# A decoder step on one core: where Pool sums the convolution's results

## The chip, the cores and the metric

The kernel runs on one core of a Trainium2 chip. The core has five engines that work side by side, each through its own instructions in their order: TensorE (PE) for matrix products, VectorE (DVE), ScalarE (ACT) and Pool (GpSimd) for elementwise work, and SyncE (SP), which here only issues transfers (DMAs). The metric is the time of one execution on the device in microseconds, the lower the better.

## The reference

One inference step of a hybrid decoder with two layers, served to a prompt group (512 positions) and a sample group (8 sequences of 4 positions) that share the weights. The model width is 1024. Layer 0 mixes with a Conformer convolution, layer 1 with an S5 state-space scan; each layer goes on with a cross-attention to memory keys and values and an MLP. The change lies in the mixer of layer 0:

```python
def _conformer_conv(u, buf, w_in, b_in, dw, dw_b, ln_g, ln_b, w_out):
    h = jnp.einsum('bld,de->ble', u, w_in) + b_in
    g = h[..., :D_MODEL] * jax.nn.sigmoid(h[..., D_MODEL:])
    padded = jnp.concatenate([buf.astype(g.dtype), g], axis=1)
    c = lax.conv_general_dilated(padded, dw[:, None, :], ...) + dw_b   # depthwise, width 31
    mu = jnp.mean(c32, axis=-1, keepdims=True)
    var = jnp.mean(jnp.square(c32 - mu), axis=-1, keepdims=True)
    n = (c32 - mu) * lax.rsqrt(var + EPS) * ln_g + ln_b
    s = jax.nn.silu(n)
    return jnp.einsum('bld,de->ble', s, w_out), padded[:, -CONV_BUF:]
```

Beside it stand `k = mem @ w_k` and `v = mem @ w_v` for both layers, whose results are outputs too; they hang on nothing in the mixer.

## The kernel before

Activations lie with channels on the 128 partitions and 544 columns (512 prompt positions and 32 sample positions) in the free dimension, so the 1024 channels are eight tiles, numbered 0 to 7. Every product is made exact to fp32 by splitting weight and activation into a high and a low half and adding three products. A weight block (128x1024) lands in one of six `wst` tiles; `prep_block` copies its high half on ACT (L137) into one of three `whl` tiles and makes the low half by a subtraction at L177, on DVE or, for the blocks named in `lpool`, on Pool. The blocks of the first projection (`ldma`) instead get their low half by an adding DMA that Pool issues (L175).

The convolution layer is a list of steps, one after another, in the order of the string `PLAN`. `a4`, `b4` are the two projections of channel tile 4 on PE, `g4` its gate. Tiles 1, 2, 4, 5 and 7 are then convolved on PE by Toeplitz matrices: `f4` fetches the tile in another layout, `40` to `43` are its four Toeplitz products (L682), and `r4` gathers the result from DRAM by four DMAs (L672). The matrices are built on Pool (L655), into two buffers in turn: the products of one step issue the building of the matrix for the step after next. Tiles 0, 3 and 6 are convolved on DVE, tap by tap in PSUM (L702), in portions that the numbers in brackets grant. The sample positions of every tile are multiplied on Pool (L632). `k` is a step of the memory's keys and values (L450, L467), which fills PE meanwhile.

Each of the results of tiles 0 to 6 is added into the tile `acc` on Pool by `conv_sum` (L622 for the first, L624 for the others), and the call stands right behind the DMAs of the gather, or behind the last instruction of a tile on DVE. The result of tile 7 is not added.

`L1` is the first step of the LayerNorm. `layernorm1` sums `acc` and the result of tile 7 over the channels by a product with ones (L714); DVE then subtracts the mean from the eight tiles (L723), ACT squares them, and Pool and DVE sum the squares (L729, L735). `L1b`, `L2`, `L2b` and `L3` go on with it, with `k` steps in between. `run` readies weight blocks ahead of the step that uses them: as a rule two, at a step with `deep=1`, as `L1`, three, before the step's own instructions are issued, if a `whl` tile is free. At `L1` the third tile is that of the `k` step just before.

Of the kernel before, what the change touches and what calls it, by code (L numbers as in the profile page):

```python
# [57 lines left out]
class Trunk:  # L58
# [7 lines left out]

    PLAN = """
        k S k s k g0 F a1 (4.2) b1 (1.5) g1 f1 a2 (4.2) b2 (1.5) g2 10 (1.8) f2 11 (1.8) a3 (4.2) 12 (1.8) b3 (1.5) g3 13 (1.8) r1 20 (1.8)
        a4 (4.2) 21 (1.8) b4 (1.5) g4 22 (1.8) f4 a5 (4.2) 23 (1.8) b5 (1.5) g5 r2 40 (1.8) f5 a6 (4.2) 41 (1.8) b6 (1.5) g6 42 (1.8)
        43 (1.8) a7 (4.2) r4 50 (1.8) b7 (1.5) g7 51 (2) f7 52 (2) V k (2) 53 k (2) r5 70 (2) k (2) 71 (2) k (2) 72 k 73 r7 k k k L1 k L1b W k k L2 k L2b O L3 k E """  # L70

    def __init__(self, nc, tc, pool, psum, I, O):
        self.nc, self.tc, self.I, self.O = nc, tc, I, O
# [429 lines left out]
    def conv_layer(self):  # L503
        nc, I, O = self.nc, self.I, self.O
        self.gp = [None] * KT
        self.nacc = 0
        self.tg, self.td = {}, {}
        st = {}
        kvb = self.mm[2]
# [61 lines left out]
        def ln1():  # L571
            while self.bgq:
                self.pop_first()
            self.layernorm1()

        def end():
# [7 lines left out]
        S = self.steps  # L584
# [9 lines left out]
        def outs():  # L594
            for f in self.late:
                f()
            self.unhold(st["v"])

        named = {"O": outs, "L1b": self.layernorm1b, "V": vbank, "F": free, "W": vbank2, "L1": ln1, "L2": self.layernorm2, "L2b": self.layernorm2b, "L3": self.layernorm3, "E": end, "S": start_stat, "s": start_rstd}
        for u in self.PLAN.split():  # L600
            if u in named:
                S.append(Step(named[u], deep=int(u in ("L1", "L1b", "L3"))))
# [8 lines left out]
            else:  # L611
                w, i = (u[0], int(u[1])) if u[0] in "fr" else (int(u[1]), int(u[0]))
                S.append(Step(lambda w=w, i=i: self.toep(w, i)))
        assert not fill

    def conv_sum(self, i, g, eng):
        self.gp[i] = g
        self.nacc += 1
        if i == 7:
            return  # L620
        if self.nacc == 1:
            self.nc.gpsimd.tensor_copy(self.acc, g)  # L622
        else:
            eng.tensor_add(self.acc, self.acc, g)  # L624

    def samples(self, i, gw, prod):

# [16 lines left out]
    def toep(self, what, i, q=None):  # L644


        nc = self.nc
# [10 lines left out]
        if what == "f":  # L658
# [3 lines left out]
            up, y, g = self.slot(), self.slot(), self.slot()  # L662
# [6 lines left out]
        elif what == "r":  # L669
            up, y, g, prod = self.td.pop(i)  # L670
            for q in range(4):
                nc.sync.dma_start(self.tv(g[32 * q : 32 * q + 32])[:, :, 8:],  # L672
                                  self.yd[i][:, :512].rearrange("(a r) (q j) -> q r a j", a=4, q=4)[q])
            self.conv_sum(i, g, nc.gpsimd)
        else:
            q = what
            n = order.index((i, q))
            up, y, g, prod = self.td[i]
            o = self.aux[1][:, q * 128 : q * 128 + 128]
            x = up[:, q * 128 : q * 128 + 128]  # L680
            for s in range(9):
                nc.tensor.matmul(o[:, s:], mat(n)[:, s * 128 : s * 128 + 128], x[:, : 128 - s], start=s == 0, stop=s == 8)  # L682
            build(n + 2)
            self.act(y[:, q * 128 : q * 128 + 128], o, AF.Identity, bias=tp(i)[:, 144 + q : 145 + q])
            if q == 1:
                self.samples_sum(i, g, prod)
            if q == 3:
                nc.scalar.dma_start(self.yd[i][:, :512], y[:, :512])

    def conv_tile(self, i, g, gw):  # L690

        nc = self.nc
# [6 lines left out]
        out = self.slot()  # L699
# [3 lines left out]
            yield 0.7  # L703
        self.samples_sum(i, out, prod)
        self.act(self.tv(out)[:, :, 8:], A.rearrange("p (c a) -> p a c", a=4), AF.Identity, bias=self.v(V_DWB + i))
        self.conv_sum(i, out, nc.gpsimd)
        yield 1.3

    def layernorm1(self):
# [1525 lines left out]
```

## Time and profile before

| | |
|---|---|
| median of 3 runs | 1545.18 us (1544.69 to 1546.54) |
| the profiled execution's own time | 1544.75 us |
| its span in the trace | 1543.0 us |
| PE busy | 1496.6 us (97%) |
| DVE busy | 1015.6 us (66%) |
| ACT busy | 685.0 us (44%) |
| Pool busy | 200.9 us (13%) |

The span is the trace's own measure from the first to the last instruction; 1.75 us of the execution lie around it. The convolution layer, with the filling `k` steps, lies in the first 220 us or so. In the rows further down a time in brackets is the idle time of an engine just before an instruction, and the name behind the arrow what ended it.

### The profile page before, as it was taken

The page shows a single profiled execution, that of the slowest core. Times are in us where ns is not written, and L with a number is a line of the kernel's source. Part 1 is how long each engine was busy: PE and PEld are TensorE (multiplying, and loading weights), DVE is VectorE, ACT ScalarE, POOL GpSimd, SP SyncE. Part 2 cuts the span into 40 slices and gives each one's busy share as a digit, 9 for nine tenths or more (in the row PEclk, how much of TensorE's full clock was granted, in tenths as well). Part 3 has the DMA queues.
Part 4 walks back from the last instruction along what each step waited for, and adds up shares of the span by engine and source line. Part 5 has one row for each costly group of instructions (what it writes and reads, how often), then busy time and mean ns, then how long its engine had stood idle before and what let it go on. Part 6 is the DMA issues. An engine that isn't in the chain of part 4 may idle for free.

```text
span 1543.0 us, 29397 instructions
## 1 busy us (share of the span) xinstructions
PE 1496.6 (97%) x11949; PEld 1450.0 (94%) x11949; DVE 1015.6 (66%) x2094; ACT 685.0 (44%) x1274; POOL 200.9 (13%) x167
## 2 busy tenths in 40 slices
PE   8999979999999999999999999999999999999996
PEld 8999969898999999999998899998899999999996
DVE  6896786444576666666757964553479677685855
ACT  6332354343445433665443443343357445272642
POOL 2555550000000000000103750000000000000001
PEclk9999989999999999999999999999999999999998
DMA  8765526453223344433587974237322314141211
GB/s 278 191 156 136 185 82 219 150 220 133 101 83 103 134 134 134 134 134 116 170 271 226 340 237 182 110 138 271 125 69 85 135 55 151 42 146 47 92 46 59
DMA packets 92535, 224.49 MB, mean 145 GB/s; under 512 B 12496, under 2 KB 42976, under 8 KB 88304
## 3 DMA queue, kind: packets, MB, share of 16 engines
q1 hardware_dynamic: 87440, 211.06, 40.1%
q0 software_dynamic: 1792, 6.37, 2.3%
q10 hardware_dynamic: 3168, 5.18, 0.9%
q8 instruction: 94, 1.54, 0.4%
q14 instruction: 41, 0.34, 0.1%
HBM read 192.78 MB, written 29.80 MB: 144 GB/s over the span
## 4 chain that ended last, share of the span: by engine, by line
PE 78%; DVE 8%; ACT 1%; issue 1%; DMA 1%; POOL 0%; SPq 0%; DVEq 0%; POOLq 0%; ACTq 0%
PE banks L215 44%; PE banks L1403 12%; PE banks L1295 10%; PE banks L467 2%; PE banks L956 2%; PE banks L892 2%; PE banks L973 1%; PE banks L876 1%; PE banks L227 1%; PE banks L1382 1%; DVE banks L1958 1%; ACT slot L137 1%; DVE banks L702 1%; PE banks L1992 1%; PE banks L1780 0%
## 5 line engine op out<-in xcount | busy, mean ns | idle before, releaser
L215 PE MATMUL banks<-slot,whl 128*128 128x272 f32 x6264 | 805.0, 290 | 6.1 <-ACT slot L137 2.9
L215 PEld LDWEIGHTS banks<-slot,whl 128*128 128x128 f32 x6264 | 794.0, 189 | 11.4 <-ACT slot L137 4.8
L137 ACT ACTIVATE whl<-wst 128x1024 fp32r<-128x1024 f32 (+1 forms) x236 | 218.7, 930 | 132.8 <-PE banks L1403 47.8
L177 DVE TENSOR_TENSOR whl<-wst,whl 128x1024 fp32r<-128x1024 f32 x137 | 169.6, 1242 | 92.8 <-ACT whl L137 91.0
L1403 PE MATMUL banks<-slot,whl 128*128 128x272 f32 x912 | 120.2, 288 | 0.5 <-DVE rt L1316 0.5
L137 ACT ACTIVATE slot<-banks 128x512 fp32r<-128x512 f32 (+7 forms) x132 | 60.3, 480 | 135.5 <-PE banks L215 42.3
L1403 PEld LDWEIGHTS banks<-slot,whl 128*128 128x128 f32 x912 | 116.7, 188 | 0.7 <-DVE rt L1316 0.7
L1295 PE MATMUL banks<-slot,whl 128*128 128x272 f32 x756 | 97.2, 288 | 0.9 <-DVE tmp L1413 0.9
L1295 PEld LDWEIGHTS banks<-slot,whl 128*128 128x128 f32 x756 | 95.6, 188 | 1.1 <-ACT whl L137 1.1
L137 ACT ACTIVATE slot<-x,vec 128x544 fp32r<-128x544 f32 (+2 forms) x50 | 35.2, 727 | 108.7 <-DVE x L2027 43.8
L1413 DVE TENSOR_TENSOR tmp<-banks,rb 128x544 f32<-128x544 f32 x30 | 21.7, 724 | 83.0 <-PE banks L1403 83.0
L1403 PE MATMUL banks<-slot,arena_mlp 128*128 128x272 f32 x528 | 71.5, 288 | 0.4 <-DVE rt L1316 0.4
L1485 POOL MEMSET slot<- 128x128 f32 x1 | 0.2, 205 | 546.9 <-PE banks L1295 546.9
L702 DVE SCALAR_TENSOR_TENSOR banks<-slot,vec,banks 128x512 f32<-128x512 f32 x90 | 67.9, 755 | 2.8
L1403 PEld LDWEIGHTS banks<-slot,arena_mlp 128*128 128x128 f32 x528 | 68.2, 188 | 0.6 <-DVE rt L1316 0.6
L1295 PE MATMUL banks<-slot,arena_mlp 128*128 128x272 f32 x504 | 65.3, 288 | 0.4 <-DVE acc L1330 0.4
L1295 PEld LDWEIGHTS banks<-slot,arena_mlp 128*128 128x128 f32 x504 | 63.9, 188 | 0.7 <-DVE acc L1330 0.6
L137 ACT ACTIVATE tmp<-x 128x544 f32<-128x544 f32 x40 | 25.9, 648 | 65.0 <-DVE x L1099 39.7
L425 POOL TENSOR_TENSOR slot<-slot,slot 128x512 fp32r<-128x512 f32 x4 | 6.1, 1557 | 371.4 <-ACT slot L137 371.4
L137 ACT ACTIVATE tmp<-banks 128x544 f32<-128x544 f32 x32 | 19.9, 623 | 76.5 <-PE banks L215 76.5
L177 POOL TENSOR_TENSOR whl<-wst,whl 128x1024 fp32r<-128x1024 f32 x19 | 45.2, 2383 | 55.2 <-ACT whl L137 55.2
L250 DVE TENSOR_TENSOR slot<-tmp,slot 128x544 fp32r<-128x544 f32 x32 | 23.2, 726 | 41.5 <-ACT slot L137 41.5
(283 smaller groups left out, 2068.8 us busy)
## 6 DMA issues: line engine op xcount, KB each, us to landing
wst<-in_w SPq DMA_DIRECT2D x231, 512.0 KB, 4.4
arena_att<-in_kc SPq DMA_DIRECT2D x16, 1024.0 KB, 4.9
arena_att<-in_vc SPq DMA_DIRECT2D x16, 1024.0 KB, 5.3
tab<-arena_prep SPq DMA_DIRECT2D x24, 512.0 KB, 3.9
whl<-in_w POOLq DMA_DIRECT2D x12, 512.0 KB, 6.2
arena_s<-tab SPq DMA_DIRECT2D x8, 768.0 KB, 5.5
arena_s<-tab SPq DMA_DIRECT2D x8, 512.0 KB, 6.3
arena_s<-tab SPq DMA_DIRECT2D x12, 256.0 KB, 5.2
```

Of the source, the lines that this page charges most:

```text
L137: self.nc.scalar.activation(out, in_, func, **kw)
L177: eng.tensor_sub(t[:, 1].bitcast(F32R), src, t[:, 0])
L215: self.nc.tensor.matmul(ps[:, c, :HALF], w, x[:, c * HALF : c * HALF + HALF], start=first and n == 0, stop=last and n == len(seq) - 1)
L227: self.nc.tensor.matmul(ps[:, c, :HALF], self.w8(b, kt)[wi], rhs[kt][xi].bitcast(F32R)[:, c * HALF : c * HALF + HALF], start=first and kt ...
L250: self.nc.vector.tensor_sub(l.bitcast(F32R), src_h if src_l is None else src_l, h)
L467: nc.tensor.matmul(ps[m], self.memt(2 * kp + k2, xi)[:, m * 128 : m * 128 + 128], t[:, wi, k2 * 512 : k2 * 512 + 512], start=kp == 0 and k ...
L702: nc.vector.scalar_tensor_tensor(A, win(k), w(k), A, op0=ALU.mult, op1=ALU.add)
L892: nc.tensor.matmul(o, qs[qi], ks[ki], start=e == 0 and i == 0, stop=e == 1 and i == 2)
L956: nc.tensor.matmul(ps[e], vs[vi], xs[xi], start=m == 0 and i == 0, stop=m == 1 and i == 2)
L1295: nc.tensor.matmul(bank, u[:, wi, k * 128 : k * 128 + 128], x[k][xi].bitcast(F32R), start=n == k == 0, stop=n == 2 and k == 3)
L1403: nc.tensor.matmul(ps[:, c, :HALF], us[kt // 4][:, wi, kt % 4 * 128 : kt % 4 * 128 + 128], M["h"][kt][xi].bitcast(F32R)[:, c * HALF : c * ...
L1413: job("V", 0.7, lambda: V.tensor_mul(self.c2(t), self.psv(ps), self.c2(self.rb)), [*bk, "rb"], [("t", o % 2)])
```

## The change

`conv_sum` is replaced by `conv_sums`. Where a result was added into `acc` at once, it is now put on a list, `pend`, and the adds for all that is on the list are issued where `PLAN` has a new mark, `+`, and once more at the beginning of `L1`. There are three marks: before `f4`, before `a7`, and behind `53`. The number of instructions is the same on every engine, and the results are added in the same sequence as before (tiles 0, 1, 3, 2, 4, 5, 6).

```diff
-        a4 (4.2) 21 (1.8) b4 (1.5) g4 22 (1.8) f4 a5 (4.2) ...
-        43 (1.8) a7 (4.2) r4 50 (1.8) b7 (1.5) g7 51 (2) f7 52 (2) V k (2) 53 k (2) r5 70 (2) k ...
+        a4 (4.2) 21 (1.8) b4 (1.5) g4 22 (1.8) + f4 a5 (4.2) ...
+        43 (1.8) + a7 (4.2) r4 50 (1.8) b7 (1.5) g7 51 (2) f7 52 (2) V k (2) 53 + k (2) r5 70 (2) k ...
@@ def ln1
             while self.bgq:
                 self.pop_first()
+            self.conv_sums()
             self.layernorm1()
@@ 
-    def conv_sum(self, i, g, eng):
-        self.gp[i] = g
-        self.nacc += 1
-        if i == 7:
-            return
-        if self.nacc == 1:
-            self.nc.gpsimd.tensor_copy(self.acc, g)
-        else:
-            eng.tensor_add(self.acc, self.acc, g)
+    def conv_sums(self):
+        for i, g in self.pend:
+            self.gp[i] = g
+            if i == 7:
+                continue
+            self.nacc += 1
+            if self.nacc == 1:
+                self.nc.gpsimd.tensor_copy(self.acc, g)
+            else:
+                self.nc.gpsimd.tensor_add(self.acc, self.acc, g)
+        self.pend = []
@@ toep, step "r"
-            self.conv_sum(i, g, nc.gpsimd)
+            self.pend.append((i, g))
@@ conv_tile, its end
-        self.conv_sum(i, out, nc.gpsimd)
+        self.pend.append((i, out))
```

Only Pool's order changes; below, a line number of the changed kernel is that of before plus 3 to 4. The first place is Pool around `L1`. `slot_1313` (after: `slot_1311`) is the result of tile 5, `slot_1464` (`slot_1462`) that of tile 6; the three L177 are the low halves of the value blocks of the three `k` steps behind `L1`. Before:

```order
L624 TENSOR_TENSOR acc<-acc,slot_1313 128x544
L655 TENSOR_TENSOR arena_mem<-istk,slot_233 128x1152
L624 TENSOR_TENSOR acc<-acc,slot_1464 128x544
L655 TENSOR_TENSOR arena_mem<-istk,slot_233 128x1152
L177 TENSOR_TENSOR whl_81<-wst_78,whl_81 128x1024
L177 TENSOR_TENSOR whl_82<-wst_79,whl_82 128x1024
L177 TENSOR_TENSOR whl_83<-wst_80,whl_83 128x1024
L719 MEMSET slot_1968 128x256
```

Here both adds stood ahead of the last two matrices, and so ahead of the three low halves. After:

```order
L659 TENSOR_TENSOR arena_mem<-istk,slot_233 128x1152 x2
L177 TENSOR_TENSOR whl_81<-wst_78,whl_81 128x1024
L177 TENSOR_TENSOR whl_82<-wst_79,whl_82 128x1024
L177 TENSOR_TENSOR whl_83<-wst_80,whl_83 128x1024
L627 TENSOR_TENSOR acc<-acc,slot_1311 128x544
L627 TENSOR_TENSOR acc<-acc,slot_1462 128x544
L723 MEMSET slot_1968 128x256
L733 TENSOR_TENSOR acc<-acc,slot_1961 128x544
```

Both adds now stand behind all three low halves, the last of which is readied at `L1` itself.

The second place is TensorE at the same step, with what each instruction waits for. Before, the last products of the `k` step and the first of the LayerNorm's:

```order
L467 MATMUL banks<-whl_83,arena_mem 128x512
L467 MATMUL banks<-whl_83,arena_mem 128x512 [waits DVE_49]
L467 MATMUL banks<-whl_83,arena_mem 128x512 x9
L714 MATMUL banks<-acc,ones 128x272
L714 MATMUL banks<-slot_1645,ones 128x272 [waits DMAHW6_49,DMAHW7_49,DMAHW5_49,DMAHW0_49]
```

The product on `acc` had no wait of its own. After:

```order
L467 MATMUL banks<-whl_83,arena_mem 128x512
L467 MATMUL banks<-whl_83,arena_mem 128x512 [waits DVE_49]
L467 MATMUL banks<-whl_83,arena_mem 128x512 x9
L718 MATMUL banks<-acc,ones 128x272 [waits Pool_49]
L718 MATMUL banks<-slot_1644,ones 128x272 [waits DMAHW6_49,DMAHW7_49,DMAHW5_49,DMAHW0_49]
```

The product on `acc` now waits for Pool.

The third place is Pool between `43` and `70`, where `slot_1143` is the result of tile 4. Before:

```order
L655 TENSOR_TENSOR arena_mem<-istk,slot_233 128x1152
L624 TENSOR_TENSOR acc<-acc,slot_1143 128x544
L655 TENSOR_TENSOR arena_mem<-istk,slot_233 128x1152 x2
L632 TENSOR_TENSOR slot_1646<-slot_242,vec 128x496
L632 TENSOR_TENSOR slot_1647<-slot_242,vec 128x496
L655 TENSOR_TENSOR arena_mem<-istk,slot_233 128x1152 x2
```

The add of tile 4 stood between the matrices of the second and third product of tile 5. After, from the last matrix ahead of the second mark on (`slot_960` and `slot_782` are the results of tiles 3 and 2):

```order
L659 TENSOR_TENSOR arena_mem<-istk,slot_233 128x1152
L627 TENSOR_TENSOR acc<-acc,slot_960 128x544
L627 TENSOR_TENSOR acc<-acc,slot_782 128x544
L659 TENSOR_TENSOR arena_mem<-istk,slot_233 128x1152 x2
L636 TENSOR_TENSOR slot_1645<-slot_242,vec 128x496
L636 TENSOR_TENSOR slot_1646<-slot_242,vec 128x496
L659 TENSOR_TENSOR arena_mem<-istk,slot_233 128x1152 x2
L627 TENSOR_TENSOR acc<-acc,slot_1143 128x544
```

The adds of tiles 3 and 2 moved to where tile 4's stood, and tile 4's moved behind the next two pairs of matrices.

## Rows read from the trace of the kernel before

**Rows 1.** The first lines of the profile's page: the span, and each engine's busy time with its share of the span and its number of instructions.

```profile
span 1543.0 us, 29397 instructions
...
PE 1496.6 (97%) x11949; PEld 1450.0 (94%) x11949; DVE 1015.6 (66%) x2094; ACT 685.0 (44%) x1274; POOL 200.9 (13%) x167
```

**Rows 2.** The waits of TensorE from 40 to 190 us, the stage in which the convolution's partial sums are formed: who waited for whom, us in total, times, the longest in us.

```profile
PE banks L682 <- ACT slot L137: 3.3, 4, 1.7
```

**Rows 3.** The same view of TensorE from 185 to 235 us, the LayerNorm of the convolution and the first products behind it.

```profile
PE banks L333 <- DVE sm_y L325: 4.6, 1, 4.6
PE banks L287 <- DVE slot L735: 2.7, 1, 2.7
```

**Rows 4.** The waits of Pool from 85 to 200 us, the row of its adds into `acc` (L624).

```profile
POOL acc L624 <- DMA slot<-yd: 22.0, 4, 6.3
```

**Rows 5.** The timeline of Pool alone: start in us, duration in us, engine, line, operation, output and inputs, how many in a row, and in brackets its idle time before them with what ended it. L655 builds a Toeplitz matrix, L624 adds a result into `acc`, L177 makes the low half of a weight block, L729 is the LayerNorm's first sum of squares.

```profile
138.46 2.13 POOL L655 TENSOR_TENSOR arena_mem<-istk,slot 128x1152 f32<-128x1152 f32 x1
145.50 1.35 POOL L624 TENSOR_TENSOR acc<-acc,slot 128x544 f32<-128x544 f32 x1 [4.92 <-DMA slot<-yd]
...
161.30 2.13 POOL L655 TENSOR_TENSOR arena_mem<-istk,slot 128x1152 f32<-128x1152 f32 x1 [1.43 <-PE banks L682]
169.74 1.34 POOL L624 TENSOR_TENSOR acc<-acc,slot 128x544 f32<-128x544 f32 x1 [6.31 <-DMA slot<-yd]
171.03 2.13 POOL L655 TENSOR_TENSOR arena_mem<-istk,slot 128x1152 f32<-128x1152 f32 x1
173.38 2.42 POOL L624 TENSOR_TENSOR acc<-acc,slot 128x544 f32<-128x544 f32 x1 [0.22 <-ACT whl L137]
...
190.95 2.40 POOL L177 TENSOR_TENSOR whl<-wst,whl 128x1024 fp32r<-128x1024 f32 x1 [0.41 <-ACT whl L137]
193.29 0.31 POOL L719 MEMSET slot<- 128x256 f32 x1
193.78 2.81 POOL L729 TENSOR_TENSOR acc<-acc,slot 128x544 f32<-128x544 f32 x2 [0.18 <-ACT slot L137]
196.54 2.40 POOL L177 TENSOR_TENSOR whl<-wst,whl 128x1024 fp32r<-128x1024 f32 x1
```

**Rows 6.** The timeline of all engines around the step `L1`, in the same columns (PEld is the weight load of a product). L467 are the products of the memory values, L714 the four products that sum the convolution's results over the channels, L723 the subtraction of the mean, L735 the rest of the sums of squares, L287 their sums over the partitions, L333 the broadcast of the result.

```profile
181.14 8.64 PE L467 MATMUL banks<-whl,arena_mem 128*128 128x512 f32 x36
...
189.38 0.42 PEld L714 LDWEIGHTS banks<-acc,ones 128*128 128x128 f32 x2
...
189.82 1.06 ACT L137 ACTIVATE whl<-wst 128x1024 fp32r<-128x1024 f32 x1 [1.74 <-PE banks L467]
...
191.25 6.91 PE L467 MATMUL banks<-whl,arena_mem 128*128 128x512 f32 x28
191.65 5.14 DVE L723 SCALAR_TENSOR_TENSOR slot<-banks,slot 128x544 f32<-128x544 f32 x8 [7.09 <-PE banks L714]
...
196.71 7.28 DVE L735 TENSOR_TENSOR slot<-slot,slot 128x544 f32<-128x544 f32 x4
...
204.05 0.38 PE L287 MATMUL banks<-ones,slot 128*128 128x2 f32 x2 [2.68 <-DVE slot L735]
...
214.21 1.11 PE L333 MATMUL banks<-ident,sm_y 128*128 128x128 f32 x4 [4.64 <-DVE sm_y L325]
```

**Rows 7.** The timeline of VectorE alone. L702 is one tap of the convolution in PSUM, L177 the low half of a weight block, L438 the low half of a memory key.

```profile
140.58 1.22 DVE L177 TENSOR_TENSOR whl<-wst,whl 128x1024 fp32r<-128x1024 f32 x1
...
162.35 2.16 DVE L177 TENSOR_TENSOR whl<-wst,whl 128x1024 fp32r<-128x1024 f32 x1
164.44 0.41 DVE L438 TENSOR_TENSOR slot<-slot,slot 128x256 fp32r<-128x256 f32 x1
...
168.48 3.12 DVE L702 SCALAR_TENSOR_TENSOR banks<-slot,vec,banks 128x512 f32<-128x512 f32 x4
...
173.36 1.23 DVE L177 TENSOR_TENSOR whl<-wst,whl 128x1024 fp32r<-128x1024 f32 x1 [0.16 <-ACT whl L137]
174.51 1.58 DVE L438 TENSOR_TENSOR slot<-slot,slot 128x256 fp32r<-128x256 f32 x1
```

**Rows 8.** The timeline of ScalarE alone: the sigmoid of the last channel tile's gate and the eviction of a Toeplitz product behind it, and further on the eviction of a finished convolution tile.

```profile
152.94 0.75 ACT L137 ACTIVATE slot<-slot,vec 128x544 f32<-128x544 f32 x1 [7.29 <-DVE slot L525]
153.59 0.35 ACT L137 ACTIVATE slot<-banks,slot 128x128 f32<-128x128 f32 x1
...
171.70 0.69 ACT L137 ACTIVATE slot<-banks,vec 128x512 f32<-128x512 f32 x1 [5.25 <-DVE banks L702]
...
173.75 0.38 ACT L137 ACTIVATE slot<-banks,slot 128x128 f32<-128x128 f32 x1
```

**Rows 9.** The timeline of TensorE alone: two of the Toeplitz products (L682) before which it waited.

```profile
154.09 2.24 PE L682 MATMUL banks<-slot,arena_mem 128*128 128x128 f32 x18 [1.73 <-ACT slot L137]
...
174.28 2.24 PE L682 MATMUL banks<-slot,arena_mem 128*128 128x128 f32 x18 [0.52 <-ACT slot L137]
```

**Rows 10.** Busy time by stretch of the span: the stretch, its length, then busy us and number of instructions of PE, PEld, DVE, ACT and POOL, the granted clock of TensorE as a share of full speed, the DMA share and GB/s.

```profile
212.00:214.00 2.00, 0.00 (x0) 0.00 (x0) 1.83 (x6) 0.00 (x0) 1.13 (x1) 0.57 0.01 2
214.00:215.00 1.00, 0.79 (x4) 0.79 (x5) 0.16 (x1) 0.00 (x0) 0.00 (x0) 0.50 0.00 0
218.00:219.00 1.00, 1.00 (x4) 0.81 (x3) 0.97 (x2) 1.00 (x2) 0.00 (x0) 0.50 0.00 0
219.00:220.00 1.00, 1.00 (x6) 0.79 (x6) 1.00 (x3) 0.29 (x2) 0.00 (x0) 0.94 0.00 0
```

More of the change, by code (lines that the diff above doesn't have):

```diff
@@ L68 @@
         k S k s k g0 F a1 (4.2) b1 (1.5) g1 f1 a2 (4.2) b2 (1.5) g2 10 (1.8) f2 11 (1.8) a3 (4.2) 12 (1.8) b3 (1.5) g3 13 (1.8) r1 20 (1.8)
-        a4 (4.2) 21 (1.8) b4 (1.5) g4 22 (1.8) f4 a5 (4.2) 23 (1.8) b5 (1.5) g5 r2 40 (1.8) f5 a6 (4.2) 41 (1.8) b6 (1.5) g6 42 (1.8)
-        43 (1.8) a7 (4.2) r4 50 (1.8) b7 (1.5) g7 51 (2) f7 52 (2) V k (2) 53 k (2) r5 70 (2) k (2) 71 (2) k (2) 72 k 73 r7 k k k L1 k L1b W k k L2 k L2b O L3 k E """
+        a4 (4.2) 21 (1.8) b4 (1.5) g4 22 (1.8) + f4 a5 (4.2) 23 (1.8) b5 (1.5) g5 r2 40 (1.8) f5 a6 (4.2) 41 (1.8) b6 (1.5) g6 42 (1.8)
+        43 (1.8) + a7 (4.2) r4 50 (1.8) b7 (1.5) g7 51 (2) f7 52 (2) V k (2) 53 + k (2) r5 70 (2) k (2) 71 (2) k (2) 72 k 73 r7 k k k L1 k L1b W k k L2 k L2b O L3 k E """
     def __init__(self, nc, tc, pool, psum, I, O):
@@ L505, in conv_layer @@
         self.gp = [None] * KT
-        self.nacc = 0
+        self.nacc, self.pend = 0, []
         self.tg, self.td = {}, {}
@@ L597, in outs @@
             self.unhold(st["v"])
-        named = {"O": outs, "L1b": self.layernorm1b, "V": vbank, "F": free, "W": vbank2, "L1": ln1, "L2": self.layernorm2, "L2b": self.layernorm2b, "L3": self.layernorm3, "E": end, "S": start_stat, "s": start_rstd}
+        named = {"O": outs, "L1b": self.layernorm1b, "V": vbank, "+": self.conv_sums, "F": free, "W": vbank2, "L1": ln1, "L2": self.layernorm2, "L2b": self.layernorm2b, "L3": self.layernorm3, "E": end, "S": start_stat, "s": start_rstd}
         for u in self.PLAN.split():
```

## The prediction

> **What bounds the kernel now.** I read the busy shares first: PE is busy for 97% of the span, DVE for 66%, Pool for 13% [rows 1]. So a change on Pool moves the time only where PE waits for it, directly or by way of another engine. Next come PE's waits in the stage where the results are formed: all that another engine ends there are 3.3 us in four waits before Toeplitz products, each ended by ACT [rows 2]. Pool, by contrast, stands still for 22.0 us in four waits of its adds for gathered results [rows 4]. That is the idle time which the change takes aim at, and nothing on PE is charged to it: the last such wait, 6.31 us before 169.74, delays a matrix to 171.03 + 2.13 = 173.16, while the product that uses it starts at 174.28 [rows 5, 9]. The matrix is ready 1.1 us early even so. Last comes the LayerNorm behind 185 us. There PE waits 2.7 and 4.6 us, both times for DVE [rows 3], and DVE's work there is one chain that starts with the products on `acc`: DVE stands idle for 7.09 us until L714 is done and then goes on to L723 and L735 [rows 6]. So in that stage the chain from `acc` onward sets the time, and PE only fills in.
>
> **What the earlier mark positions give.** Pool no longer waits for gathers between matrices, so matrices come up to 4.9 us sooner. PE had no wait for them, so I put this at 0. The most that could come back is the 3.3 us of [rows 2], but those waits end with ACT, and ACT is held by DVE in the two cases that I show: the eviction at 153.59 stands behind a sigmoid that waited for DVE, and that at 173.75 behind an eviction that waited for DVE's last tap [rows 8]. PE starts at 154.09 and 174.28 right behind them [rows 9].
>
> **What the moved adds do to DVE.** For the same reason a delay of DVE before 171.6 reaches PE in full. The rows show that DVE and Pool hold each other up on such work: DVE's L177 takes 1.22 us by itself and 2.16 us at 162.35, where Pool builds a matrix until 163.43; at 173.38 Pool's add, due just behind the start of a DVE L177, takes 2.42 us instead of 1.34, and DVE's L438 behind that L177 then takes 1.58 us instead of 0.41 [rows 5, 7]. At the third mark the add of tile 4 comes right behind the matrix of 161.30, that is at 163.4, when DVE's L177 is under way. This is the scene of 173.38 again: the add waits for the L177, and L438 at 164.44 waits for the add. Cost on DVE: 1.58 − 0.41 = 1.2 us, which the taps that end at 168.48 + 3.12 = 171.6 pass on to ACT and PE. At the second mark two adds come right behind the matrix of 138.46, that is at 138.46 + 2.13 = 140.6, and DVE's next L177 starts at 140.58 [rows 5, 7]. Who is first there is within a few hundredths of a microsecond: if Pool, DVE loses 1.3 us (one add), if DVE, nothing. I take half, 0.6, and keep 0 and 1.3 for the range. The sum of both is **+1.8 us** (0 to 2.5; 0 if the third mark misses DVE's work too).
>
> The Trainium skill (GPSIMD Engine Reference, 8. Key points) says that GpSimd shares its SBUF interfaces with VectorE and contends with those VectorE instructions that have two SBUF inputs or run in a two-port mode. L177 and L438 have two such inputs, so by that rule both places collide and the term would be 2.5; the trace agrees as to L177 and L438, but leaves open at 140.58 which of the two engines pays.
>
> **What the adds at the beginning of `L1` do.** Here lies most of the cost. At `L1` the low half of a third weight block is issued on Pool ahead of the step's own instructions, and its `whl` tile is free only when PE has done the `k` step just before. The rows give the sequence: PE's products end at about 189.4, ACT copies the high half at 189.82 [1.74 <-PE], Pool makes the low half from 190.95 on [rows 5, 6]. Before, nobody on the chain waited for that; the adds of tiles 5 and 6 had been done at 169.74 and 173.38. Now these two adds are queued behind it, and L714 waits for them. Pool is through with the low half at 193.29 (the start of the next instruction). An add takes 1.29 us from start to start (169.74 to 171.03) and 1.34 by its record, and DVE has nothing to do meanwhile, so nothing stretches them: 193.29 + 1.29 + 1.34 = 195.9. With 0.1 us for the handover (ACT's copy ends at 189.82 + 1.06 = 190.88, Pool starts at 190.95) L714 starts at 196.0 instead of 189.38 [rows 6]: **+6.6 us** (6.4 to 6.8). PE can't fill the gap: its instructions go in order, and the filling `k` step stands behind L714. SP's loads and ACT's next work stand behind nothing new. What is late next is the whole chain: L723, L735, L287, then L333 and the first products of the output projection. Pool's own next work, the memory set and L729, waited for ACT's squares at 193.78 anyway [0.18 <-ACT], and these move with L723.
>
> **What the gap does to PE's clock.** After the wait of 4.64 us before 214.21 the granted clock is 0.57 in 212 to 214 and 0.50 (1.2 of 2.4 GHz) until 219, and then 0.94 [rows 6, 10]. A gap of 6.6 us is longer, so I expect L714 to start at half the clock. At full clock its loads and products take from 189.38 to 191.25, where the next products start: 1.9 us. At half the clock they take twice that: **+1.9 us** on the chain (0.9 if the clock returns midway, 2.0 if all of it is slow). The `k` products behind them are slower too for a few microseconds, but that is covered by PE's wait of 2.68 us before L287 [rows 6].
>
> The Trainium skill (TensorE: Matmul & The Clock Gate, Part 1, What's actually happening) holds that low speed is the resting state, which activity lifts, and that the number of matmuls that run at low speed differs from one execution to the next. No row here shows two executions; by that statement the term is a spread and not a constant, as the two ends above already have it.
>
> **The sum.** 0 + 1.8 + 6.6 + 1.9 = 10.3 us on the profiled execution's own 1544.75 us, which gives 1555.05. The median of the three runs lies 0.43 us above that execution, so I say 1555.5. Nothing later takes the loss back: from 220 us on PE's work stands behind this chain, and the loads are issued as weight tiles come free, so they shift with it.
>
> **Rivals.**
> 1. *Only the wait.* The marks don't meet DVE's work, and the clock is back midway in L714: 6.6 + 0.9 = 7.5 us, 1552.7. For it: a shift of half a microsecond parts Pool and DVE. Against it: the scene of 173.38 fits the third mark closely.
> 2. *The wait, and more.* Both marks cost DVE in full (2.5), L714 is slow throughout (2.0), and the later pieces of the chain on PE, L287 and L333, which run at either clock, fall badly by another 1.5: 6.6 + 6.0 = 12.6, 1557.8.
> 3. *Not slower: PE's later waits pay.* PE idles 2.68 + 4.64 = 7.3 us before L287 and L333 [rows 6]. If these waits were ended by something that doesn't hang on L714, 6.6 us would fit into them, and the time stays at 1545 to 1546. What could do so is Pool's work: the L177 of 196.54 lies on the first of the four L735, which take 7.28 us, so DVE may wait there for Pool and not for the mean. The point from which this decides is whether Pool's low halves move with L714. They stand behind L729, which needs the squares behind L723, so they do; and if a changed meeting spares DVE one such L177, that saves 2 us, not 6.
> 4. *Faster.* The freed Pool lets PE's 3.3 us of waits go, and the adds at `L1` come in time: 1541.9. It needs the third low half to be done before PE reaches L714, though it starts when PE is done.
>
> **How the numbers follow.** Chances: the forecast 0.68, rival 1 0.12, rival 2 0.10, rival 3 0.06, rival 4 0.04. About 0.2% (3.1 us) is what a measurement of this kernel can tell from no change. Rivals 1, 2 and the forecast are slower by more than that, 0.90; rival 3 is the 0.06 within, rival 4 the 0.04 faster. The range leaves out rivals 3 and 4. Its low end has no cost at the marks, 6.4 and 0.9, and 2.0 spared on an L735: 1545.18 + 5.3 = 1550.5. Its high end is rival 2 rounded up: 1558.
>
> **What would show it.** In the changed profile PE should have a wait of some 6.6 us before the products on `acc`, ended by Pool's last add, and in Pool's timeline the order low half, add, add, with no idle time between. The granted clock in those products should be about 0.5. The eviction behind the sigmoid near 153 us, and the one near 174, should come 0 to 1.3 and 1.2 to 2.5 us later, each with a longer wait of PE. DVE's idle time before the mean should grow from 7.1 to some 15 us, and the four L735 should look as before. The prediction is wrong if PE enters the products on `acc` without a wait, if the chain from there to the output projection is shorter than before, or if matrices that come earlier take waits off PE in the stage before.

## The result, and the profile after

The changed kernel takes 1554.93 us (median of 6 runs, 1553.58 to 1557.35) against 1545.36 us before in the same series. The medians differ by 9.6 us. The ratio is 1.0059 with a 95% interval of 1.0046 to 1.0071, that is 9.1 us (7.1 to 11.0). The profiled execution took 1554.10 us with a span of 1552.3 us, 9.3 us above the span of before. Of all runs in this document one, of e9 further down, took 1819.23 us, at a granted clock of 0.749 against 0.985 to 0.992 in the others, and is left out of its ratio.

First, the waits of TensorE in the changed kernel, 185 to 245 us, the view of [rows 3]: who waited for whom, us in total, times, the longest.

```profile
PE banks L718 <- DMA wst<-in_w: 6.3, 1, 6.3
PE banks L333 <- DVE sm_y L325: 6.2, 1, 6.2
PE banks L287 <- DVE slot L739: 1.8, 1, 1.8
```

There is a new wait of 6.3 us before the products on `acc` (L718 now, L714 before). The view puts it down to a weight load; that is the one releaser that came last by its reckoning, and it is wrong here, since the product on `acc` has a wait for Pool and no other. The timeline of Pool, as in [rows 5], shows what the products waited for:

```profile
141.14 3.63 POOL L627 TENSOR_TENSOR acc<-acc,slot 128x544 f32<-128x544 f32 x2
...
164.57 2.26 POOL L659 TENSOR_TENSOR arena_mem<-istk,slot 128x1152 f32<-128x1152 f32 x1 [3.28 <-PE banks L686]
166.79 1.33 POOL L627 TENSOR_TENSOR acc<-acc,slot 128x544 f32<-128x544 f32 x1
...
193.50 2.34 POOL L177 TENSOR_TENSOR whl<-wst,whl 128x1024 fp32r<-128x1024 f32 x1 [0.47 <-ACT whl L137]
195.80 2.73 POOL L627 TENSOR_TENSOR acc<-acc,slot 128x544 f32<-128x544 f32 x2
```

The third low half ran from 193.50, the two adds behind it from 195.80 for 2.73 us, to 198.53. All engines around that place, the view of [rows 6]:

```profile
192.37 1.06 ACT L137 ACTIVATE whl<-wst 128x1024 fp32r<-128x1024 f32 x1 [1.79 <-PE banks L467]
...
198.59 1.27 PE L718 MATMUL banks<-acc,ones 128*128 128x272 f32 x2 [6.31 <-DMA wst<-in_w]
...
201.99 8.08 PE L467 MATMUL banks<-whl,arena_mem 128*128 128x512 f32 x28
202.62 5.14 DVE L727 SCALAR_TENSOR_TENSOR slot<-banks,slot 128x544 f32<-128x544 f32 x8 [15.58 <-PE banks L718]
...
225.20 1.12 PE L333 MATMUL banks<-ident,sm_y 128*128 128x128 f32 x4 [6.16 <-DVE sm_y L325]
```

L718 starts at 198.59, 0.06 us behind the second add. ACT's copy at 192.37 is that of the third block. Before, the same product was this one, in TensorE's timeline there:

```profile
189.62 0.62 PE L714 MATMUL banks<-acc,ones 128*128 128x272 f32 x2
```

Counted from the start of the value products (181.14 before, 183.62 after), L718 starts 14.97 us on (198.59) where it started 8.48 us on (189.62, just behind its weight load of 189.38): **6.5 us**. Then the clock, in the view of [rows 10] (stretch, length, busy time of PE, PEld, DVE, ACT and POOL, granted clock, DMA share, GB/s):

```profile
192.00:194.00 2.00, 0.28 (x2) 0.00 (x0) 0.00 (x0) 1.06 (x1) 1.53 (x2) 1.00 1.00 399
194.00:196.00 2.00, 0.00 (x0) 0.00 (x0) 0.00 (x0) 0.00 (x0) 2.00 (x2) 0.58 1.03 422
...
200.00:202.00 2.00, 2.00 (x7) 1.43 (x5) 0.00 (x0) 0.00 (x0) 0.00 (x0) 0.50 0.00 0
...
206.00:208.00 2.00, 2.00 (x10) 1.64 (x9) 1.76 (x3) 1.58 (x3) 1.92 (x3) 1.00 0.00 0
```

PE stops in 192 to 194, the granted clock is 0.58 in 194 to 196 and 0.50 in 200 to 202, while L718 runs, and 1.00 again from 206. From L718 to the broadcast L333 it takes 225.20 − 198.59 = 26.61 us; before it was 214.21 − 189.62 = 24.59. That is **2.0 us** more. All of it lies between the product and VectorE's first subtraction of the mean: 202.62 − 198.59 = 4.03 us after, 191.65 − 189.62 = 2.03 before.

What lies ahead of that shows best on VectorE (the view of [rows 7]) and TensorE (that of [rows 9], with the product `42` as a first mark):

```profile
141.17 2.40 DVE L177 TENSOR_TENSOR whl<-wst,whl 128x1024 fp32r<-128x1024 f32 x1
...
150.48 1.22 DVE L177 TENSOR_TENSOR whl<-wst,whl 128x1024 fp32r<-128x1024 f32 x1
...
167.00 2.21 DVE L177 TENSOR_TENSOR whl<-wst,whl 128x1024 fp32r<-128x1024 f32 x1
169.13 0.41 DVE L438 TENSOR_TENSOR slot<-slot,slot 128x256 fp32r<-128x256 f32 x1
```

```profile
131.86 2.16 PE L686 MATMUL banks<-slot,arena_mem 128*128 128x128 f32 x18
...
155.76 3.25 PE L686 MATMUL banks<-slot,arena_mem 128*128 128x128 f32 x18 [2.83 <-ACT slot L137]
158.68 3.74 PE L450 MATMUL banks<-arena_mem,whl 128*128 128x256 f32 x24
162.26 2.16 PE L686 MATMUL banks<-slot,arena_mem 128*128 128x128 f32 x18
...
176.84 2.17 PE L686 MATMUL banks<-slot,arena_mem 128*128 128x128 f32 x18
```

The same marks of TensorE before, `42` and `53` (`52` and `72` are in [rows 9]):

```profile
131.26 2.16 PE L682 MATMUL banks<-slot,arena_mem 128*128 128x128 f32 x18
...
158.99 2.17 PE L682 MATMUL banks<-slot,arena_mem 128*128 128x128 f32 x18
```

VectorE's low half at the second mark takes 2.40 us where it took 1.22 at 140.58 [rows 7]; Pool's two adds begin at 141.14, 0.03 us ahead of it. Counted from product `42` (131.26 before), product `52` comes 155.76 − 131.86 = 23.90 us later, and before 22.83: +1.1 us. In this longer wait of 2.83 us the clock fell (0.69 in 156 to 158 us, 0.50 in 158 to 160): `52` takes 3.25 us instead of 2.24, the key products behind it 3.74. So `53` at 162.26 is 30.40 us behind `42`, where it was 27.73 (158.99 − 131.26): +2.7. Product `72` at 176.84 no longer waits, which gives 0.5 and a little more back. When the products on the memory's values begin, PE is 183.62 − 131.86 = 51.76 us behind `42`, before 181.14 − 131.26 = 49.88: **1.9 us** for the marks in this profile.

The sum up to L333 is 1.9 + 6.5 + 2.0 = 10.4 us behind `42`. That product itself came 0.6 us later than before. Nearly all of this is there already at the first broadcast of the kernel (L333 at 32.57 us, before at 32.00), long ahead of the first add that the change moves (tile 0's, at 79.71 before), and the start of `42` differs from profile to profile (131.3 to 133.6). From that broadcast to `42` it takes 99.3 us in both kernels, so the first mark, which lies there, moves nothing on TensorE. So L333 is 225.20 − 214.21 = 11.0 us late, yet the span is only 9.3 us longer. Some 1.5 us come back far behind, in a stretch that the change doesn't touch. The same place in both kernels, before and then after, in the view by stretch:

```profile
760.00:765.00 5.00, 4.00 (x22) 4.01 (x23) 4.79 (x11) 4.34 (x13) 0.00 (x0) 0.68 0.79 258
```

```profile
771.00:776.00 5.00, 4.04 (x33) 4.04 (x34) 4.79 (x11) 4.31 (x13) 0.00 (x0) 1.00 0.76 260
```

The products behind a wait in these stretches, from the timeline of TensorE, again before and then after:

```profile
761.00 1.22 PE L1780 MATMUL banks<-ident,arena_prep 128*128 128x128 f32 x8 [1.89 <-ACT arena_prep L137]
```

```profile
771.96 1.09 PE L1784 MATMUL banks<-ident,arena_prep 128*128 128x128 f32 x8 [1.89 <-ACT arena_prep L137]
```

PE waits there for 1.9 us in both kernels, and the changed one is 10.96 us late, as it was at L333. In this execution of before the clock fell behind that wait, in this one of after it did not: to the next group of small products (L1788 before, L1792 after) it takes 769.59 − 761.00 = 8.59 us before and 779.00 − 771.96 = 7.04 after, and the changed kernel is 9.4 us late from there.

### The profile page after: what moved, and what is told of

Same layout as the page of the kernel before. It is cut to its first block, busy times and chain, and to the rows that moved or that the text cites. A ratio compares the mean times of both kernels' runs of the same rounds, so it can differ in the third digit from the quotient of the medians.

```text
span 1552.3 us, 29394 instructions
## 1 busy us (share of the span) xinstructions
PE 1498.0 (97%) x11949; PEld 1451.3 (93%) x11949; DVE 1018.6 (66%) x2094; ACT 684.8 (44%) x1274; POOL 201.5 (13%) x167
## 4 chain that ended last, share of the span: by engine, by line
PE 80%; DVE 6%; ACT 1%; DMA 1%; issue 1%; POOL 0%; DVEq 0%; ACTq 0%; POOLq 0%
PE banks L215 44%; PE banks L1407 12%; PE banks L1299 10%; PE banks L467 2%; PE banks L960 2%; PE banks L896 2%; PE banks L450 1%; PE banks L977 1%; PE banks L880 1%; PE banks L227 1%; PE banks L686 1%; PE banks L1386 1%; DVE banks L1962 1%; ACT slot L137 1%; DMA arena_s<-tab 1%
## 5 line engine op out<-in xcount | busy, mean ns | idle before, releaser
L177 DVE TENSOR_TENSOR whl<-wst,whl 128x1024 fp32r<-128x1024 f32 x137 | 172.8, 1265 | 93.4 <-ACT whl L137 90.8
L177 POOL TENSOR_TENSOR whl<-wst,whl 128x1024 fp32r<-128x1024 f32 x19 | 45.5, 2398 | 59.3 <-ACT whl L137 59.3
```

The source lines that it names most:

```text
L177: eng.tensor_sub(t[:, 1].bitcast(F32R), src, t[:, 0])
```

## The experiments

Each is timed in one series with the kernel before; the medians of before in the three series are 1544.89 us (18 runs; e1 to e4 without e2b), 1545.04 us (15; e2b, e5, e6, e7) and 1545.36 us (27; e8 to e10). The changed kernel's row is the result above, with six runs of before. The table gives the start of some instructions of TensorE in each profile, counted from the start of product `42`, as the difference to the same distance before (22.83, 43.02, 58.36 and 82.95 us): `52`, `72`, the first product on `acc`, and the broadcast L333. The ratio comes from the comparison of the series as a whole and can differ from the quotient of the medians by some 0.0005. A row is read from left to right: what grows between two columns was lost between them.

| kernel | median us, ratio to before (95%) | `52` | `72` | on `acc` | L333 |
|---|---|---|---|---|---|
| changed | 1554.93, 1.0059 (1.0046 to 1.0071) | 1.1 | 2.0 | 8.4 | 10.4 |
| e1_mark_r7 | 1548.95, 1.0025 (1.0015 to 1.0035) | 1.1 | 3.3 | 3.3 | 3.3 |
| e2_two_late | 1554.10, 1.0064 (1.0052 to 1.0077) | −0.1 | 1.1 | 7.5 | 9.5 |
| e2b_two_late_again | 1554.33, 1.0059 (1.0046 to 1.0071) | −0.1 | 1.1 | 7.6 | 9.6 |
| e3_marks_moved | 1545.61, 1.0006 (0.9997 to 1.0015) | −0.1 | 1.1 | 1.1 | 1.5 |
| e4_pe_busy | 1554.05, 1.0062 (1.0050 to 1.0075) | 1.1 | 3.2 | 9.6 | 9.6 |
| e5_third_half_dve | 1553.57, 1.0057 (1.0043 to 1.0070) | 1.1 | 2.3 | 6.8 | 8.8 |
| e6_two_late_busy | 1552.80, 1.0044 (1.0031 to 1.0058) | −0.1 | 1.1 | 7.9 | 8.3 |
| e7_fifth_in_place | 1546.08, 1.0003 (0.9994 to 1.0012) | −0.1 | −0.1 | −0.1 | −0.1 |
| e8_products_first | 1545.48, 1.0002 (0.9993 to 1.0010) | 0.0 | 0.0 | 0.0 | 0.2 |
| e9_all_marks_products_first | 1544.83, 1.0000 (0.9991 to 1.0009) | 0.0 | 0.0 | 0.1 | 0.1 |
| e10_second_mark_moved | 1545.43, 1.0005 (0.9996 to 1.0014) | −0.1 | 1.1 | 1.1 | 1.6 |

**The late adds taken out.** One mark more, so that the adds of tiles 5 and 6 stand ahead of the three low halves:

```diff
-... 72 k 73 r7 k k k L1 ...
+... 72 k 73 r7 + k k k L1 ...
```

> One more mark, behind the gather of tile 7, so that the adds of tiles 5 and 6 stand ahead of the three low halves again; all else as changed. Theory (the adds behind the third low half hold the LayerNorm's first products for 6.5 us, and the clock that falls in that gap costs 1.8 us more): both go, 1554.9 - 8.3 = 1546.6 us (1545.5 to 1548.0), with TensorE's longer wait near 155 us still there. Rival (the loss is in the marks further ahead, where the adds meet VectorE's work, and the late adds only take from waits that TensorE had anyway): 1553 us or more.

The time falls to 4.1 us above before, and nothing is lost between `72` and L333 any more. So most of the loss was the late adds. What is left is more than expected. VectorE's and then TensorE's timeline in this kernel:

```profile
142.95 2.41 DVE L177 TENSOR_TENSOR whl<-wst,whl 128x1024 fp32r<-128x1024 f32 x1
...
166.21 2.36 DVE L438 TENSOR_TENSOR slot<-slot,slot 128x256 fp32r<-128x256 f32 x1
...
171.86 2.36 DVE L438 TENSOR_TENSOR slot<-slot,slot 128x256 fp32r<-128x256 f32 x1
```

```profile
133.64 2.16 PE L686 MATMUL banks<-slot,arena_mem 128*128 128x128 f32 x18
...
157.55 3.63 PE L686 MATMUL banks<-slot,arena_mem 128*128 128x128 f32 x18 [2.81 <-ACT slot L137]
...
179.94 2.24 PE L686 MATMUL banks<-slot,arena_mem 128*128 128x128 f32 x18 [1.32 <-ACT slot L137]
...
195.28 0.62 PE L718 MATMUL banks<-acc,ones 128*128 128x272 f32 x2
```

The second mark costs the same as in the changed kernel (2.41 us for the low half; `52` waits 2.81 us and then runs slow, 3.63 us). In addition L438 takes 2.36 us where it took 0.41, twice, and `72` at 179.94 waits 1.32 us. The products on `acc` start without a wait. Up to `72` the instructions and their order are those of the changed kernel, whose profile has 2.0 us there and this one 3.3; this is taken up again below.

**The late adds alone.** The kernel before, with only these two adds put off to `L1`:

```diff
-def conv_sum(self, i, g, eng):
+def conv_sum(self, i, g, eng, late=False):
     self.gp[i] = g
+    if i in (5, 6) and not late:
+        self.pend.append((i, g, eng))
+        return
@@ ln1
+            for p in self.pend:
+                self.conv_sum(*p, late=True)
             self.layernorm1()
```

> The kernel before, with only the adds of tiles 5 and 6 put off to the beginning of the LayerNorm's first step; the others stay right behind their gathering. Theory: a wait of 6.5 us and 1.8 us for the low clock, 1545.4 + 8.3 = 1553.7 us (1552.5 to 1555.0). Rival (TensorE's two later waits of 7.3 us together pay for it): 1545 to 1547 us. Rival (the loss lies in the marks): 1545.4 us.

It takes 9.2 us more than before; the rivals' 1545 to 1547 us are out. From `72` to the product on `acc` it loses 7.5 − 1.1 = 6.4 us, from there to L333 2.0. A second series with the same kernel gives 9.3 us:

> The kernel before with only the adds of tiles 5 and 6 put off, once more, as the partner of the run with idle products: 9.2 us above before, as at first (8.5 to 9.9).

In that profile the view of TensorE's waits names the right releaser:

```profile
PE banks L719 <- POOL acc L629: 6.3, 1, 6.3
```

The 1.1 us ahead of `72` was not expected: none of the marks is in this kernel. It is taken up again below.

**All marks moved.** On top of the first experiment:

```diff
-... f5 a6 (4.2) 41 (1.8) b6 (1.5) g6 42 (1.8) 43 (1.8) + a7 (4.2) r4 50 (1.8) b7 ... 53 + k ...
+... f5 a6 (4.2) 41 (1.8) + b6 (1.5) g6 42 (1.8) 43 (1.8) a7 (4.2) r4 50 (1.8) + b7 ... 53 k ...
```

> The extra mark of the run before this, and the second and third mark moved to places where VectorE either waits for TensorE (behind the second product of tile 4) or works on PSUM taps (behind the first product of tile 5). Theory (the adds at the second mark hold up a low half on VectorE for 1.2 us, which reaches TensorE by way of the sigmoid and the eviction, and the clock that falls in the longer wait costs another 1 to 1.5 us): 1.2 to 2.5 us below the kernel with the extra mark alone, 1545.0 us (1544.0 to 1546.0), and the wait near 155 us back at 1.7 us. Rival (where the adds stand ahead of the LayerNorm makes no difference): the same time as with the extra mark alone.

The loss at `52` is gone, and with it 3.3 us of the median. The 1.1 us at `72` is there as in the second experiment. VectorE's and Pool's timelines show why, here in this kernel:

```profile
167.98 2.37 DVE L177 TENSOR_TENSOR whl<-wst,whl 128x1024 fp32r<-128x1024 f32 x1
```

```profile
167.13 2.14 POOL L659 TENSOR_TENSOR arena_mem<-istk,slot 128x1152 f32<-128x1152 f32 x1 [2.73 <-PE banks L686]
```

The same low half before, in the timeline of VectorE there:

```profile
167.01 1.22 DVE L177 TENSOR_TENSOR whl<-wst,whl 128x1024 fp32r<-128x1024 f32 x1
```

Pool stood still then, waiting for the gather of tile 5 until 169.74 [rows 5]. Here the low half takes 2.37 us. Nothing holds Pool any more, so its matrix for `72` comes at 167.13, just ahead of that low half. In both profiles of the late adds alone, where tile 5's add is put off too, that low half takes 2.37 us as well. The next experiment tests this.

**Tile 5's add back in its place.** One mark more on top of the one before:

```diff
-... 53 k (2) r5 70 (2) ...
+... 53 k (2) r5 + 70 (2) ...
```

> The kernel with all marks moved, and one mark more behind the gather of tile 5, so that Pool waits for that gather ahead of the matrix for the third product of tile 7, as before the change. Theory (that wait kept Pool off a low half which VectorE makes meanwhile; without it the matrix and the low half meet, VectorE loses 1.1 us, and so does TensorE before the first product of the next pair): the low half takes 1.2 us again instead of 2.4, TensorE's wait near 175 us falls from 1.7 to 0.5 us, and the time is that of before, 1.0 us below the kernel with all marks moved: 1544.7 us (1544.0 to 1545.4). Rival (Pool's wait had no effect on others): as with all marks moved, 0.7 us above before.

VectorE and Pool in that kernel:

```profile
168.72 1.22 DVE L177 TENSOR_TENSOR whl<-wst,whl 128x1024 fp32r<-128x1024 f32 x1
```

```profile
163.01 2.14 POOL L659 TENSOR_TENSOR arena_mem<-istk,slot 128x1152 f32<-128x1152 f32 x1 [1.32 <-PE banks L686]
172.03 1.35 POOL L627 TENSOR_TENSOR acc<-acc,slot 128x544 f32<-128x544 f32 x1 [6.88 <-DMA slot<-yd]
```

Pool waits 6.88 us for the gather again, the low half takes 1.22 us, and from `42` to L333 the kernel is as fast as before (−0.1 us in each column). The median, with an interval of −0.9 to +1.9 us, can't tell 1 us; here the trace decides, and not the time.

**TensorE kept at work in the gap.** The changed kernel, with products that nobody reads:

```diff
             self.conv_sums()
+            for _ in range(7):
+                nc.tensor.matmul(self.aux[1], self.ones, self.rb[:, :512], start=True, stop=True)
             self.layernorm1()
```

> The changed kernel, with seven more products of 128x512 (of ones with a tile that is at rest, into a PSUM bank that nobody reads) in front of the LayerNorm's products, so that TensorE works through the gap of 6.5 us; they take some 6.0 us at full clock and do no work of the reference. Theory (the low clock in the LayerNorm's products costs 1.8 us on the chain): the granted clock stays at full, the four pairs of products take 1.9 us instead of 3.4, and the time falls by 1.8, to 1553.1 us (1552.3 to 1553.8). Rival (that slowness is hidden, as TensorE waits for VectorE later anyway): 1554.9 us, no difference.

TensorE in that kernel:

```profile
156.96 4.17 PE L688 MATMUL banks<-slot,arena_mem 128*128 128x128 f32 x18 [2.81 <-ACT slot L137]
...
201.00 0.72 PE L720 MATMUL banks<-acc,ones 128*128 128x272 f32 x2 [0.26 <-POOL acc L629]
...
225.64 1.11 PE L333 MATMUL banks<-ident,sm_y 128*128 128x128 f32 x4 [4.63 <-DVE sm_y L325]
```

From the product on `acc` to L333 it takes 225.64 − 201.00 = 24.64 us, the 24.59 of before. But the time is 9.2 us above before, against 9.6, and the intervals of the two ratios overlap: the expected 1.8 us don't show. In the profiled execution, which was the slowest of the five, the trace tells where part of them went: the fall of the clock at `52` was longer (4.17 us for `52`), and `72` came 1.2 us later than in the changed kernel's profile. So I repeated it on the kernel with the late adds alone, in which the clock doesn't fall at `52`, in one series with it:

> The kernel before with only the adds of tiles 5 and 6 put off, and the seven idle products in front of the LayerNorm's (they do no work of the reference), beside the same kernel without these products in one series. Theory (the low clock costs 2.0 us between the first product on the sum and the broadcast, as the trace of the changed kernel shows it, and half of it comes back later, since the clock then happens to rise sooner behind the broadcast): 0.8 to 2.0 us below the run without them. Rival (all of it is hidden or given back): no difference, within 0.4 us.

1552.80 us (1551.23 to 1553.07) against 1554.33 us (1553.90 to 1555.44): 1.5 us, with no overlap of the five runs each, though the intervals of the two ratios overlap. In the profiles, the loss from `acc` to L333 falls from 2.0 to 0.5 us; from the product on `acc` to VectorE's first subtraction it takes 2.14 us, where the changed kernel took 4.03 and before 2.03. The 0.5 us that are left come later, and e3 and e10, which have no gap, show them too. The gap's clock is on the path.

**The third low half on VectorE.** In the changed kernel:

```diff
-... {("v", 0, 1, k) for k in range(4)} ...
+... {("v", 0, 1, k) for k in (0, 2, 3)} ...
```

> The changed kernel, with the third low half (the value block readied at the LayerNorm's first step) made by VectorE instead of Pool; the adds of tiles 5 and 6 then stand behind the second low half only. Theory (what holds the adds is that half at the head of Pool's queue): they start 2.8 us earlier, where they meet VectorE's new instruction and lose up to 1.2 us to it, so the wait of 6.3 us before the products on the sum falls to 3.5 to 4.7 us and the time by 1.6 to 2.8, to some 1552.7 us (9.2 us above before becomes 6.5 to 7.8). Rival (the adds wait for something else, a gather or a load): the wait stays at 6.3 us and the time at 1554.9 us.

All engines there:

```profile
192.77 3.60 POOL L627 TENSOR_TENSOR acc<-acc,slot 128x544 f32<-128x544 f32 x2
193.19 2.00 DVE L177 TENSOR_TENSOR whl<-wst,whl 128x1024 fp32r<-128x1024 f32 x1 [6.37 <-ACT whl L137]
...
196.43 1.28 PE L718 MATMUL banks<-acc,ones 128*128 128x272 f32 x2 [4.37 <-POOL acc L627]
```

The adds start right behind the second low half, 192.77, and meet VectorE's new low half, as expected: 3.60 us for the two, and 2.00 for the half. The wait is 4.37 us. From `72` to the product on `acc` the loss is 4.5 us instead of 6.4. The time, 8.5 us above before, is less changed than expected (6.5 to 7.8), and by the intervals it can't be told from that of the changed kernel; the trace shows the effect, and not the time. The half at the head of Pool's queue is what holds the adds.

This profile also shows something about the marks. Up to `72` it has the order of the changed kernel, and `52` waits just as long:

```profile
155.16 2.24 PE L686 MATMUL banks<-slot,arena_mem 128*128 128x128 f32 x18 [2.79 <-ACT slot L137]
```

But here the clock did not fall (1.00 from 154 to 166 us, and 2.24 us for `52`). Then the third mark does cost what the prediction had for it: the low half of a key at 165.55 takes 1.55 us instead of 0.41, and `72` is 2.3 us late, 1.1 from `52` and 1.2 more.

**The second mark by itself.** The first experiment with only the second mark moved, as above:

```diff
-... 41 (1.8) b6 (1.5) g6 42 (1.8) 43 (1.8) + a7 ...
+... 41 (1.8) + b6 (1.5) g6 42 (1.8) 43 (1.8) a7 ...
```

> The kernel with the extra mark behind tile 7's gather, and the second mark alone moved to where VectorE waits; the third mark stays as in the change. Theory (the extra mark alone cost 4.1 us, of which the second mark's meeting with a low half makes 1.2, the clock that fell in the longer wait 1.4, and the third mark's meeting with the low half of a key 1.1): TensorE's wait near 155 us is 1.7 us again and the clock stays up there, the third mark still costs 1.1 us: 1545.0 + 1.2 = 1546.2 us (1545.5 to 1546.9). Rival (the third mark costs nothing, as in the profile of the changed kernel): 1545.0 us.

VectorE there:

```profile
140.75 1.22 DVE L177 TENSOR_TENSOR whl<-wst,whl 128x1024 fp32r<-128x1024 f32 x1
...
164.50 1.55 DVE L438 TENSOR_TENSOR slot<-slot,slot 128x256 fp32r<-128x256 f32 x1
```

The low half at the second mark's old place takes 1.22 us, `52` is not late; the key's low half at 164.50 takes 1.55 us instead of 0.41, as the prediction had it for the third mark, and `72` is 1.1 us late. Tile 5's missing wait is not the cause of that here: the low half that it exposes, at 168.21, takes 1.25 us, as Pool's matrix, begun at 166.25, was nearly done by then. The median is 0.1 us above before, less than that; with an interval of −0.6 to +2.2 us it can't tell.

**A version meant to beat both.** The kernel before, with a portion of tap work ahead of `42` and not behind it, and then the same on top of the kernel with tile 5's add in its place:

```diff
-... g6 42 (1.8) 43 (1.8) ...
+... g6 (1.8) 42 43 (1.8) ...
```

> The kernel before, with one edit: the portion of tap work behind the third product of tile 4 is granted ahead of that product, so that Pool's products for tile 6's samples stand ahead of the Toeplitz matrix that used to meet VectorE's evacuation of tile 6. Theory (a Pool instruction that meets a VectorE instruction with two SBUF inputs between 131 and 172 us costs TensorE time by way of VectorE): VectorE saves up to 2.2 us there, TensorE's wait of 1.7 us near 154 us falls to 0 to 0.5 us and that of 0.5 us near 174 goes, and the time falls by 1.2 to 2.2 us, to some 1543.3 us. Rival (the taps and low halves behind it meet Pool's matrices a little later instead, and the gain is spent): 1544.5 to 1545.5 us.

> The kernel with all marks moved and the mark behind tile 5's gather, plus the same edit of the tap work. Theory: as the run before this, 1543.3 us, since these marks stand where VectorE doesn't mind them. Rival: the adds of tile 4 or the matrices, which come sooner here, meet the earlier VectorE work, and the time is 1544.5 us or more.

Both are the same as before within 0.1%. VectorE in the first of them:

```profile
134.07 0.25 DVE L538 SCALAR_TENSOR_TENSOR slot<-slot,vec,slot 128x32 f32<-128x32 f32 x1
...
138.89 3.10 DVE L177 TENSOR_TENSOR whl<-wst,whl 128x1024 fp32r<-128x1024 f32 x1
```

The instruction at 134.07 takes 0.25 us where the matrix used to meet it (2.10 us at 133.98 before), so the first half of the theory held. But the low half behind it now comes at 138.89, into two matrices in a row, and takes 3.10 us instead of 1.22. What was won is spent: the rival. No version here beats the kernel before.

## Why the prediction was right, point by point

- **The marks bring TensorE nothing.** Right. In the experiments that take the late adds away no distance is shorter than before by more than 0.1 us. Taking Pool's waits for gathers away shortened nothing on TensorE.
- **The late adds hold the products on the sum for 6.6 us.** Right: 6.5 us, and 6.4 us with these adds alone. It went the way the rows said: ACT's copy, the third low half, two adds. VectorE's idle time before the mean is 15.58 us, as foretold. One reading was off, with nothing resting on it: PE's products end at 181.14 + 8.64 = 189.78 [rows 6], not at 189.4. Rival 3 (PE's later waits pay) is out: these waits move with the chain and are 1.8 and 6.2 us, 8.0 together, where they were 7.3.
- **The clock costs 1.9 us on the chain.** Right: 2.0 us from the products to VectorE's first subtraction, gone but for 0.1 us when TensorE is kept at work (e4, e6).
- **The marks cost 1.8 us.** The sum fits the changed kernel's profile (1.9 us), but its terms do not, so the agreement is luck. The second mark was taken at half of 1.3 us, as a tie; Pool was first and VectorE paid 1.2 us in all four profiles in which the mark stands there (2.39 to 2.41 us for the low half in the changed kernel, e1, e4 and e5). The Trainium skill (GPSIMD Engine Reference, 8. Key points), by which both marks collide, was nearer at this one. The clock at `52` was not in the sum at all: in the longer wait of 2.8 us it fell in the changed kernel, 1.6 us more, and in e1 and e4, but not in e5. And the prediction charged 1.2 us to the third mark, which in the changed kernel's profile doesn't reach TensorE, and the longer wait that it expected near 174 us is missing. The matrix ahead of that add stood behind `53`, which was 2.7 us late, so the add came at 166.79 and not at 163.4 and met another low half (2.21 us at 167.00), while the low half that had met a matrix before (2.16 us at 162.35) was spared. And PE, already late, no longer waits for ACT at `72`. In e5 and e10, where the clock didn't fall, the third mark costs 1.2 and 1.1 us. With the same instructions in the same order up to `72`, the four profiles are 2.0, 3.3, 3.2 and 2.3 us late there: the term is a spread, and all four lie above the 1.8.
- **What it missed.** Pool's idle time in the gather of tile 5 was worth something to another engine: it kept a matrix off a low half of VectorE, 1.1 us at `72`, shown by taking that wait away (e2, e3) and putting it back (e7). The parts therefore don't add up: e1 costs 4.1 us and the late adds alone 9.2 us, together 13.3, but the change 9.6. In the profiles 2.4 us of the difference lie ahead of `72` (3.3 and 1.1 us, against 2.0): 1.1 is the cost of the missing wait, which is missing in all three kernels and so is counted twice, and 1.3 is what e1 and the changed kernel differ by with the same instructions.
- **Nothing later takes the loss back.** Nothing of the change does: the changed kernel is 11.0 us late at L333 and 10.96 at 772 us. The single profile is 1.5 us better than the sum for another reason, a fall of the clock behind 761 us that came in one execution and not in the other.

What stays open is how often each of these small meetings happens from run to run: the runs of one kernel spread over 1.5 us (five of e2b) to 5.4 us (27 of before), and one profile shows one case.

## What to carry to other kernels

Before work is put off to a later mark, look at what will stand ahead of it in its engine's queue there: here the queue held an instruction that could not start until TensorE had finished the step before, and so did everything behind it. A wait that costs its own engine nothing can still shelter another engine with which it shares something; taking it away is a change of its own. And where a kernel's runs spread by a few microseconds, distances between two instructions in the trace settle effects of 1 us that the medians can't, if more than one profile has the stretch: here four profiles of the same instructions gave 2.0 to 3.3 us.

## What the runs showed of the hardware

- In these rows Pool and VectorE take turns instruction by instruction. Where Pool's two adds came 0.03 us ahead of VectorE's low half, VectorE took 2.40 instead of 1.22 us, 1.2 more, about one add, and the pair of adds took 3.63 us, which is 0.9 us more than the 2.73 of the undisturbed pair at 195.80: VectorE got in between them. Who paid first was settled by a lead of a few hundredths of a microsecond: before the change, VectorE's low half began 0.02 us ahead of Pool's add at 173.38, took 1.23 us, and the add 2.42 instead of 1.34 [rows 5, 7].
- A wait of TensorE of 1.9 us (ended at 761.00 before, at 771.96 after) was followed by a fall of the clock in one profile (0.68 in 5 us) and not in another (1.00), a difference of 1.5 us for the same instructions. The Trainium skill (TensorE: Matmul & The Clock Gate, Part 1, What's actually happening) says that the number of matmuls at low clock at a kernel's start differs from execution to execution; these two rows, from the middle of two kernels, show the like. A wait of 2.8 us before `52` was followed by such a fall in three profiles (`52` took 3.25, 3.63 and 4.17 us) and not in a fourth (2.24). How much of the spread of a kernel's runs comes from this is not shown.
